# A transformer block on one core: where the pre-added weight sums of a seven-product matrix multiply are made and kept

## The chip, the cores and the metric

The kernel runs on one core of one Trainium2 chip. The metric is the device time of one execution in microseconds (us), as the median of several runs. A core has a matrix engine (TensorE, PE in the profile; its weight loads are PEld), a vector engine (VectorE, DVE), a scalar engine (ScalarE, ACT), a general engine (GpSimd, POOL) and a fifth one that here only issues transfers (SyncE, SP). Each engine works through its own instructions in order and waits on semaphores for the others.

## The reference, cut to what matters

One layer on 256 tokens of width 2048: an input projection, a gated delta rule branch, a sparse attention branch, two sigmoid gates, an output projection, a layer norm, and a gated feed-forward of width 5632 with a second layer norm. All in fp32.

```python
proj = x @ w_in[l]
(qkv_a, a_in, b_in, z, q_b, k_b, v_b, q_i, k_i, w_i, gate_a, gate_b) = jnp.split(proj, offsets, axis=-1)
...
merged = jax.nn.sigmoid(gate_a) * (o_a @ w_branch_a[l]) + jax.nn.sigmoid(gate_b) * (o_b @ w_branch_b[l])
x = layer_norm(DEEPNORM_ALPHA * x + merged @ w_out[l], ln1_g[l], ln1_b[l])
h_gate, h_up = jnp.split(x @ w_ffn_in[l], 2, axis=-1)
x = layer_norm(DEEPNORM_ALPHA * x + (jax.nn.silu(h_gate) * h_up) @ w_ffn_out[l], ln2_g[l], ln2_b[l])
```

## The kernel before

Every weight element is used once, so the weights stream from memory in chunks of 128 x 1024 (512 KB). A chunk is split into a rounded part `hi` (ScalarE, L91) and the remainder `lo` (VectorE, L93); a product with fp32 accuracy is then three matmuls (activations' hi with weights' hi, hi with lo, lo with hi; `mm3`, L217 to L219). Four chunk buffers of each kind (`raw`, `hi`, `lo`) let loading and splitting run ahead of TensorE.

The large projections work on *groups* of 1024 output columns. A group's inner dimension of 2048 is cut into eight *pairs* (numbered q = 0 to 7) of 256 rows. With the 256 tokens as two halves and the 1024 columns as two halves, a pair is a 2 x 2 by 2 x 2 block product. A *plain* pair does its eight block products, 24 matmuls (`plain_pair`). A *seven-product* pair does seven, 21 matmuls (`seven_pair`), after Winograd's form of Strassen's scheme: it needs sums of the weight blocks (`t13`, `t24`: L246, L250, L251 on VectorE), split in turn (L241, L242), and sums of the inputs (`x_form`, made once per q). Four accumulators of the other PSUM pool (`wbank`; the pools `acc` and `aux` have four banks each, and swap roles from group to group) hold the four products that enter several outputs; after the last seven-product pair of a group they are combined (`sums_chain`, L1065 to L1072) and added to the plain ones.

If a pair's weight sums are *ready*, that is made and split earlier, `seven_pair` only needs one and a half chunks split. The sums can be made ready in three ways:

- `early_sums`: just ahead, from the same loads (in z, the gates and the output projection).
- *near*: during group 1 of the feed-forward's first projection (the second large projection stage; groups 1 to 10, tensor `wfg`), for pair 0 of groups 2 and 3, into tiles that group 1 does not need yet (in `f_forms_chain`, four sums by `four_sums`, L934 to L939, and a split, L209).
- *kept*: long ahead, during the first projection (`wws`, `win`), for pair 0 of groups 4 to 7 (`kept_chain`): the two chunks are loaded by SyncE (L948), summed in place, split (L958, L959), and stored by GpSimd's queue to a scratch tensor `d_s` (L961, L962). Before the group that uses them, `kept_load` loads the four tiles back by SyncE (L1415).

Which pairs are seven-product ones: `ZQ` for z, `GQ` for the four gate groups, `FQ` for groups 1 to 10; `ZO`, `GO`, `FO` give the order in which a group takes its pairs, where it is not 0 to 7.

The orders on TensorE and SyncE are written out by hand: they are the order of the program text. Helper work is interleaved by *chains*, generators that `tick` advances at each chunk (a `yield n` waits n ticks, a `yield "name"` an event). The orders on VectorE, ScalarE and GpSimd are chosen when the program is built, by a planner with priorities (`tc.high_priority(offset=LEAD)` raises them; the kept sums have `-LEAD`) and estimated times, and are then fixed.

The stages in order: first projection (to about 356 us; the kept chain runs from `KEPT_FROM` ticks on), z group, gate groups 0 and 1, the attention branch's projection `wbb`, gate groups 2 and 3, the delta branch's projection `wba`, output projection, first layer norm, the feed-forward's first projection (`wfi`, then groups 1 to 10 of `wfg`), its second one (`wfo`), second layer norm.

Of the kernel before, what the change touches and what calls it, by code (L numbers as in the profile page):

```python
# [8 lines left out]
F32 = mybir.dt.float32  # L9
# [8 lines left out]
P = 128  # L18
# [21 lines left out]
GQ = ((2, 4, 6), (0, 2, 4, 6), (0, 2, 4, 6), (0, 2, 4, 6))  # L40
GO = (range(8), (1, 0, 3, 2, 5, 4, 6, 7), (1, 3, 2, 4, 5, 6, 0, 7), (1, 0, 3, 2, 5, 4, 6, 7))
OO = (1, 3, 0, 2, 5, 4, 6, 7)
ZQ = (2, 4, 6)
ZO = (0, 1, 3, 2, 4, 5, 6, 7)
OQ = (0, 2, 4, 6)
WALL = sorted({*WQ[0], *WQ[1]})
KEPT = (4, 5, 6, 7)
NEAR = (2, 3)
FQ = ((4, 6), *[(0, 2, 4, 6) if i in KEPT + NEAR else (2, 4, 6) for i in range(2, 11)])
FO = (1, 3, 2, 0, 4, 5, 6, 7)  # L50
KEPT_FROM = 56
OUT_AT = (8, 9, 10)

LN2_LOAD = (5, 7, 9, 11)
# [9 lines left out]
def block_kernel(ctx: ExitStack, tc: tile.TileContext, xT, x, cpack, onehot, relb, convw, alog, dtb, gnw,  # L64
# [35 lines left out]
    def start(gen, at_once=False):  # L100
        chains.append([gen, clock[0] + (next(gen) if at_once else 0)])
# [17 lines left out]
    def event(name):  # L119
        done[name] = clock[0]  # L120
# [220 lines left out]
    def T(name, shape, dtype=F32, tag=None):  # L341
        return p1.tile(shape, dtype, name=name, tag=tag or name)
# [62 lines left out]
    def need(*names):  # L405
        for n in names:
            assert n in done, n
# [519 lines left out]

    d_s = dr.tile([len(KEPT), 2, P, 2, 1024], F32, name="d_s")

    def four_sums(ra, rb, lead=0):  # L930

        r0, r1, s0, s1 = (t[:, n * 512:n * 512 + 512] for t in (ra, rb) for n in range(2))
        with tc.high_priority(offset=lead):
            nc.vector.tensor_add(r0, r0, s1)  # L934
            nc.vector.tensor_add(s1, r1, s1)
        yield 1
        with tc.high_priority(offset=lead):
            nc.vector.tensor_add(r1, r0, r1)
            nc.vector.tensor_add(s0, r1, s0)  # L939

    def kept_chain():
        yield KEPT_FROM
        raws = [T("k_raw", [P, 2, 1024], tag=t) for t in ("oh_", "s_x")]
        hi = T("k_hi", [P, 2, 1024], F32R, tag="ol_")
        for m, g in enumerate(KEPT):
            raw = raws[m % 2]
            for i in range(2):
                nc.sync.dma_start(raw[:, i], wfg[g - 1, i])  # L948
                yield 1
            yield 1  # L950
            for _ in four_sums(raw[:, 0], raw[:, 1], -LEAD):
                yield 1
            yield 1
            for i in range(2):
                with tc.high_priority(offset=-LEAD):
                    for n in range(2):
                        cs = slice(n * 512, n * 512 + 512)
                        nc.scalar.copy(hi[:, i, cs], raw[:, i, cs])  # L958
                        nc.vector.tensor_sub(raw[:, i, cs].bitcast(F32R), raw[:, i, cs], hi[:, i, cs].bitcast(F32))  # L959
                yield 1  # L960
                nc.gpsimd.dma_start(d_s[m, 0, :, i], hi[:, i].bitcast(F32))  # L961
                nc.gpsimd.dma_start(d_s[m, 1, :, i], raw[:, i])  # L962
        event("kept")

    start(kept_chain())
    conv_first(s_kT, pss)
    event("kc0")
    for dst, h0, c0, ev in ((s_kT, 4, 12, "kc1"), (s_qT, 0, 0, "qc0"), (s_qT, 4, 4, "qc1"),
# [24 lines left out]
    def z_chain():  # L993

        yield "v1"
        yield 1
        need("kept")
        t0 = [rp.tile([P, 2, 1024], F32R, name=f"z_t{i}", tag=f"x1_{i}") for i in range(2)]
        wt = two("z_wt", F32, "ol_")
        gates_home.update(wraw=halves(two("z_wraw", F32, "oh_")), wt=halves(wt), thi=halves(t0[0]), tlo=halves(t0[1]))  # L1000
        for q, old in ((4, "s_ak"), (6, "s_sq")):
            t = T(f"g_form{q}", [P, 2, 4, P], F32R, tag=old)
            gates_form[q] = t[:, 0], t[:, 1]
        gates_form[2] = [p1.tile([P, 4, P], F32R, name="g_form2", tag="rel", bufs=2) for _ in range(2)]
        yield from early_sums(wz, ZQ[0], home, z_ready)
        yield 1
        x_form(ZQ[0], gates_form[ZQ[0]], wt[:, 0, :512], wt[:, 0, 512:])
        yield "lg"
        t1 = two("z_t2", F32R, "s_vT"), two("z_t3", F32R, "s_t")
        for tag, *t in zip(("thi", "tlo"), t0, t1):  # L1010
            gates_home[tag] = halves(*t)
            gates_home[tag][0] = 2
        yield from early_sums(wz, ZQ[1], home, z_ready)
        for q in ZQ[1:]:
            yield 1
            x_form(q, gates_form[q], wt[:, 0, :512], wt[:, 0, 512:])
        event("zready")
# [30 lines left out]
    def next_sets(*olds):  # L1048
        for tag, old in zip(("thi", "tlo"), olds):
            e = gates_home[tag]  # L1050
            gates_home[tag] = [0, e[1][:2] + halves(two("h_" + old, F32R, old))[1]]
# [88 lines left out]

    def ga_rows():
        if "a" not in g_rows:
            next_sets("s_x", "s_mn")
            g_rows["a"] = [rp.tile([P, D], F32, name=f"ga{tb}", tag=f"x1_{tb}") for tb in range(NTB)]
        return g_rows["a"]
# [4 lines left out]
    token_block(vb, 1)  # L1150
    event("vb")
    need("lg", "o", "mask")
    z_group()
    event("z")
    gates_buffers()
    start(late_form(0))
    for i in range(2):
        gate_group(gb_rows, i)
    gb = gb_rows()
    for tag in ("thi", "tlo"):  # L1160
        gates_home[tag][0] = 0
    start(early_chain(wgt[2], (2, 4), ga_ready, "gaready"))
    for j in range(4):
        js = slice(j * 512, (j + 1) * 512)
        for tb, ps in enumerate(block_xs([wbb[j, k] for k in range(4)], *out_hl, ps_acc if j == 2 else ps_aux)):
            nc.vector.tensor_mul(gb[tb][:, js], ps, gb[tb][:, js])
# [85 lines left out]
    def fetch(i, j):  # L1252
# [1 line left out]
        nc.sync.dma_start(t.rearrange("p k t -> p (k t)").bitcast(F32), d_h[i, j])  # L1254

    h_first = passing()
    near = [[hp_.tile([P, 1024], F32R if i > 1 else F32, name="near", tag=f"{hl}{i}") for hl in ("hH", "hL")]
            for i in range(1, 5)]
    l1 = ExitStack()
    gp = l1.enter_context(tc.tile_pool(name="gp1", bufs=1, side="left", reuse_waits="tile"))  # L1260
    ex = l1.enter_context(tc.tile_pool(name="ex1", bufs=4, side="left", reuse_waits="tile"))
# [71 lines left out]
    def fv():  # L1333
        return fp.tile([P, 512], F32, name="v", tag="v", bufs=4)
# [20 lines left out]
                  lambda tb, ps: start(h_chain(0, tb, gated(tb, ps), ps_aux)))  # L1355
    l1.close()
    hp2 = fh.enter_context(tc.tile_pool(name="hp2", bufs=1, side="left", reuse_waits="tile"))
    near.append([hp2.tile([P, 1024], F32R, name="near", tag=f"{hl}5") for hl in ("hH", "hL")])
    kept = [None, [hp2.tile([P, 1024], F32R, name="kept", tag=f"{hl}6") for hl in ("hH", "hL")]]


    f_home = {}
# [13 lines left out]
    def f_forms_chain():  # L1376
        yield "x1"
        for tb in range(NTB):
            yield 2
            nc.sync.dma_start(d_x1[tb], x1[tb])  # L1380
        t = [rp.tile([P, 2, 2, 4, P], F32R, name="f_form", tag=f"x1_{tb}") for tb in range(NTB)]
        for i, q in enumerate((4, 6, 2, 0)):
            yield 1
            f_form[q] = t[i // 2][:, i % 2, 0], t[i // 2][:, i % 2, 1]
            x_form(q, f_form[q], fv(), fv())
        yield 1
        raw = near[0]
        for m, g in enumerate(NEAR):
            for i in range(2):
                nc.sync.dma_start(raw[i], wfg[g - 1, i])  # L1390
                yield 1
            yield 1
            yield from four_sums(*raw)
            for i in range(2):
                yield 1
                split(near[1 + 2 * m][i], near[2 + 2 * m][i], raw[i])
            k_ready[g][0] = sums_of(near[1 + 2 * m], near[2 + 2 * m])
            yield 4

    k_ready = {g: {} for g in KEPT + NEAR}  # L1400

    def sums_of(hi, lo):
        (t1, t2), (t4, t3) = ([(hi[i][:, n * 512:n * 512 + 512], lo[i][:, n * 512:n * 512 + 512]) for n in range(2)]
# [3 lines left out]
    def kept_load(m):  # L1407

        for i in range(2):
            if m or not i:  # L1410
                kept[i] = [hp2.tile([P, 1024], F32R, name="kept", tag=f"{hl}{5 + i}") for hl in ("hH", "hL")]
            for j in range(2):
                if i or j:
                    yield 3
                nc.sync.dma_start(kept[i][j].bitcast(F32), d_s[m, j, :, i])  # L1415
        k_ready[KEPT[m]][0] = sums_of(*zip(*kept))

# [47 lines left out]
    for i in range(1, NG + 1):  # L1465
        std, shared = (ps_aux, ps_acc) if i % 2 else (ps_acc, ps_aux)
        sums = []

        def places():
            sums.extend(fv() for _ in range(4))  # L1470
            return sums

        at = {6: lambda: start(kept_load(KEPT.index(i + 1)))} if i + 1 in KEPT else {}
        ready = k_ready.get(i)
        if ready is not None:
            at[0] = lambda ready=ready: ready[0]
        bank = x_group(wfg[i - 1], FQ[i - 1], std, shared, f_form, fhome, lambda wbank: sums_chain(places(), wbank),
                       at, range(8) if ready is None else FO, {} if ready is None else ready)
        if i == NEAR[-1]:
            for k in range(1, 5):  # L1480
                h_tile(hp_, k)
        if i == KEPT[-1]:
            for k in (5, 6):
                h_tile(hp2, k)
        if i == NG:
            h_tile(hp2, 7)
        start(hidden_chain(i, bank, sums, std), at_once=True)
# [258 lines left out]
```

## Time and profile before

| | us |
|---|---|
| median of 3 runs | 1454.04 (1452.1 to 1454.48) |
| the profiled execution, whole | 1454.49 |
| its span on the core | 1452.7 |
| TensorE busy | 1443.7 |
| VectorE busy | 1279.0 |
| ScalarE busy | 813.9 |

The profile is of one execution. "Span" is from its first to its last instruction. Rows of the timeline give the start in us, the duration, engine, line of the kernel and operation; "x2" is the number of instructions in one row. Rows of the grouped view give the number of instructions, their busy time, the mean duration in ns, and the idle time of the engine just before them with what ended it. A row of a stretch of time gives its length and the busy us of PE, PEld, DVE, ACT and POOL with instruction counts, then the granted clock, the transfers' share and GB/s. Matmuls are pipelined, so the duration shown for one is longer than the step from one to the next.

### The profile page before, as it was taken

What the parts mean: (1) busy time and instruction counts of PE and PEld (TensorE: products, weight loads), DVE (VectorE), ACT (ScalarE), POOL (GpSimd) and SP (SyncE); (2) the same over time, 40 slices, a digit from 0 to 9 for tenths busy, and PEclk for the clock granted to TensorE, in tenths of its full rate; (3) what the DMA queues carried; (4) which work ended last, traced back from release to release, by engine and by line L of the source; (5) the groups of instructions that cost most, each with busy time, mean ns of one, the idle gap of its engine ahead of it and who ended that gap; (6) DMA issues with size and microseconds to landing.
All of it is one profiled execution on the core that took longest, in us unless ns stands there. A gap on an engine that the chain in (4) does not pass through costs nothing.

```text
span 1452.7 us, 19640 instructions
## 1 busy us (share of the span) xinstructions
PE 1443.7 (99%) x7140; PEld 1213.8 (84%) x7140; DVE 1279.0 (88%) x1763; ACT 813.9 (56%) x1021; POOL 56.2 (4%) x75
## 2 busy tenths in 40 slices
PE   9999999999999999999999999999999999999998
PEld 8888888888888888888888878888888888888887
DVE  6798988789699959998886999989999998989987
ACT  5765454557456646655435665656566565554552
POOL 0002011121000000000000000000000000000000
PEclk9999999999999999999999999999999999999999
DMA  8646589854556755756856767777766666887863
GB/s 293 197 159 196 175 216 335 295 187 151 169 198 232 233 193 198 247 188 204 304 202 218 264 236 253 251 271 255 279 211 212 216 215 247 311 342 265 315 215 118
DMA packets 101969, 336.40 MB, mean 232 GB/s; under 512 B 17696, under 2 KB 18888, under 8 KB 101360
## 3 DMA queue, kind: packets, MB, share of 16 engines
q1 hardware_dynamic: 88512, 310.03, 62.0%
q0 software_dynamic: 6176, 22.75, 4.6%
q10 hardware_dynamic: 7184, 2.36, 0.7%
q8 instruction: 56, 0.92, 0.2%
q14 instruction: 41, 0.34, 0.1%
HBM read 312.88 MB, written 22.22 MB: 231 GB/s over the span
## 4 chain that ended last, share of the span: by engine, by line
PE 92%; DVE 3%; DMA 3%; issue 1%; ACT 1%; SPq 0%; POOLq 0%; DVEq 0%; ACTq 0%
PE acc L217 10%; PE acc L218 10%; PE acc L219 10%; PE acc L153 10%; PE aux L218 9%; PE aux L217 9%; PE aux L219 9%; PE acc L156 5%; PE acc L175 3%; PE acc L173 3%; PE acc L174 3%; PE aux L173 2%; PE aux L174 1%; PE aux L175 1%; DMA raw<-in_win_dram 1%; PE aux L737 1%
## 5 line engine op out<-in xcount | busy, mean ns | idle before, releaser
L91 ACT CAST hi<-raw 128x1024 fp32r<-128x1024 f32 (+1 forms) x388 | 396.9, 1032 | 345.3 <-PE acc L219 87.3
L93 DVE TENSOR_TENSOR lo<-raw,hi 128x1024 fp32r<-128x1024 f32 (+1 forms) x388 | 463.5, 1205 | 87.3 <-ACT hi L91 84.7
L153 PE MATMUL acc<-X,hi 128*128 128x512 f32 x640 | 203.7, 400 | 0.0
L217 PE MATMUL acc<-hi,X 128*128 128x512 f32 x369 | 145.0, 393 | 0.8 <-DVE v L1072 0.8
L156 PEld LDWEIGHTS acc<-X,lo 128*128 128x128 f32 x640 | 120.2, 188 | 28.3
L219 PE MATMUL acc<-hi,X 128*128 128x512 f32 x369 | 143.7, 389 | 0.0
L218 PE MATMUL acc<-lo,X 128*128 128x512 f32 x369 | 143.6, 389 | 0.0
L156 PE MATMUL acc<-X,lo 128*128 128x256 f32 x640 | 126.0, 278 | 0.0
L217 PE MATMUL aux<-hi,X 128*128 128x512 f32 x313 | 122.4, 391 | 0.0
L219 PE MATMUL aux<-hi,X 128*128 128x512 f32 x313 | 121.9, 389 | 0.0
L218 PE MATMUL aux<-lo,X 128*128 128x512 f32 x313 | 121.8, 389 | 0.0
L153 PEld LDWEIGHTS acc<-X,hi 128*128 128x128 f32 x640 | 97.5, 189 | 2.0 <-ACT hi L91 0.7
L241 ACT CAST f_thi<-f_wt 128x1024 fp32r<-128x1024 f32 x58 | 61.0, 1053 | 46.4 <-DVE f_wt L251 23.9
L217 PEld LDWEIGHTS acc<-hi,X 128*128 128x128 f32 x369 | 69.3, 188 | 15.9 <-DVE v L1072 1.2
L219 PEld LDWEIGHTS acc<-hi,X 128*128 128x128 f32 x369 | 69.3, 188 | 14.5
L218 PEld LDWEIGHTS acc<-lo,X 128*128 128x128 f32 x369 | 69.3, 188 | 13.9
L242 DVE TENSOR_TENSOR f_tlo<-f_wt,f_thi 128x1024 fp32r<-128x1024 f32 x58 | 70.6, 1220 | 6.2 <-ACT f_thi L241 6.1
L219 PEld LDWEIGHTS aux<-hi,X 128*128 128x128 f32 x313 | 58.8, 188 | 12.3
L218 PEld LDWEIGHTS aux<-lo,X 128*128 128x128 f32 x313 | 58.8, 188 | 12.1
L217 PEld LDWEIGHTS aux<-hi,X 128*128 128x128 f32 x313 | 58.8, 188 | 12.0
L241 ACT CAST thi<-wt 128x1024 fp32r<-128x1024 f32 x36 | 37.9, 1054 | 49.0 <-DVE wt L246 31.6
L173 PE MATMUL acc<-hi,X 128*128 128x512 f32 x160 | 64.3, 402 | 0.0
(681 smaller groups left out, 3123.6 us busy)
## 6 DMA issues: line engine op xcount, KB each, us to landing
raw<-in_wfg_dram SPq DMA_DIRECT2D x125, 512.0 KB, 4.8
raw<-in_wws_dram SPq DMA_DIRECT2D x80, 512.0 KB, 4.1
raw<-in_wfo_dram SPq DMA_DIRECT2D x70, 512.0 KB, 5.0
raw<-in_wgt_dram SPq DMA_DIRECT2D x49, 512.0 KB, 3.9
f_wraw<-in_wfg_dram SPq DMA_DIRECT2D x29, 512.0 KB, 6.2
raw<-in_win_dram SPq DMA_DIRECT2D x21, 512.0 KB, 4.1
wraw<-in_wfo_dram SPq DMA_DIRECT2D x18, 512.0 KB, 5.1
gt<-d_g SPq DMA_DIRECT2D x18, 512.0 KB, 6.8
```

The costliest lines, as they stand in the source:

```text
L91: nc.scalar.copy(hi, raw)
L93: nc.vector.tensor_sub(lo, raw, hi.bitcast(F32))
L153: nc.tensor.matmul(pss[c], hv[:, kk, cs[c]], X2[k // 4][:, k % 4], start=(k == 0), stop=False, skip_group_check=True)
L156: nc.tensor.matmul(pss[c][:, :S], lv[:, kk, cs[c]], xh[:, k, :], start=False, stop=(k == KT - 1), skip_group_check=True)
L173: nc.tensor.matmul(ps, xh, hv[:, kk], start=(k == 0), stop=False)
L174: nc.tensor.matmul(ps, xh, lv[:, kk], start=False, stop=False)
L175: nc.tensor.matmul(ps, xl, hv[:, kk], start=False, stop=(k == 2 * n - 1))
L217: nc.tensor.matmul(o, sh, hi, start=first, stop=False)
L218: nc.tensor.matmul(o, sh, lo, start=False, stop=False)
L219: nc.tensor.matmul(o, sl, hi, start=False, stop=last)
L241: nc.scalar.copy(hi, v)
L242: nc.vector.tensor_sub(lo, v, hi.bitcast(F32))
```

## The change

z has four seven-product pairs instead of three, with another order, and the form of input 0 is made during z instead of after it. Group 1 has three instead of two, with an order of its own. The near sums are gone: group 2 has no ready pair and three seven-product pairs instead of four, and group 3's pair 0 becomes a kept one, so that five groups (3 to 7) have one. Four of the five are kept in the first projection, starting four ticks earlier; the fifth (group 7) runs beside `wbb`, in one raw tile and one `hi` tile. The first of each four kept sums multiplies its operand by a column of ones that SyncE loads just then, two ticks after the second raw tile. The input forms of the feed-forward get buffers of their own.

```diff
-ZQ = (2, 4, 6)
-ZO = (0, 1, 3, 2, 4, 5, 6, 7)
+ZQ = (2, 4, 0, 6)
+ZO = (1, 3, 5, 2, 4, 0, 6, 7)
...
-KEPT = (4, 5, 6, 7)
-NEAR = (2, 3)
-FQ = ((4, 6), *[(0, 2, 4, 6) if i in KEPT + NEAR else (2, 4, 6) for i in range(2, 11)])
+KEPT = range(3, 8)
+FQ = [(0, 2, 4, 6) if i in KEPT else (2, 4, 6) for i in range(1, 11)]
+F1 = (1, 3, 4, 5, 6, 0, 2, 7)
 FO = (1, 3, 2, 0, 4, 5, 6, 7)
-KEPT_FROM = 56
+KEPT_FROM = 52
...
-    def four_sums(ra, rb, lead=0):
+    def four_sums(ra, rb, lead, one):
...
-            nc.vector.tensor_add(r0, r0, s1)
+            nc.vector.scalar_tensor_tensor(r0, r0, one, s1, op0=OP.mult, op1=OP.add)
             nc.vector.tensor_add(s1, r1, s1)
...
-    def kept_chain():
-        yield KEPT_FROM
-        raws = [T("k_raw", [P, 2, 1024], tag=t) for t in ("oh_", "s_x")]
-        hi = T("k_hi", [P, 2, 1024], F32R, tag="ol_")
-        for m, g in enumerate(KEPT):
-            raw = raws[m % 2]
+    def kept_chain(ms, wait, old, old_hi, gap, ev):
+        yield wait
+        raws = [T(f"k_raw{t}", [P, 2, 1024], tag=t) for t in old]
+        hi = T(f"k_hi{old_hi}", [P, 2, 1024], F32R, tag=old_hi)
+        for m in ms:
+            if gap and m > ms[0]:
+                yield gap
+            raw = raws[m % len(old)]
             for i in range(2):
-                nc.sync.dma_start(raw[:, i], wfg[g - 1, i])
+                nc.sync.dma_start(raw[:, i], wfg[KEPT[m] - 1, i])
                 yield 1
             yield 1
-            for _ in four_sums(raw[:, 0], raw[:, 1], -LEAD):
+            one = sm.tile([P, 1], F32, name="one", tag="one", bufs=2)
+            nc.sync.dma_start(one, cpack[:, C_ONE:C_ONE + 1])
+            for _ in four_sums(raw[:, 0], raw[:, 1], -LEAD, one):
                 yield 1
...
-    start(kept_chain())
+    start(kept_chain(range(4), KEPT_FROM, ("oh_", "s_x"), "ol_", 0, "kept0"))
...
-        for q in ZQ[1:]:
+        for q in ZQ[1::2]:
...
     def ga_rows():
         if "a" not in g_rows:
+            need("kept1")
...
+    start(late_form(0))
     z_group()
     event("z")
     gates_buffers()
-    start(late_form(0))
...
     start(early_chain(wgt[2], (2, 4), ga_ready, "gaready"))
+    start(kept_chain(range(4, 5), 1, ("s_x",), "s_rv", 5, "kept1"))
...
-    near = [[hp_.tile([P, 1024], F32R if i > 1 else F32, name="near", tag=f"{hl}{i}") for hl in ("hH", "hL")]
-            for i in range(1, 5)]
+    room = [[hp_.tile([P, 1024], F32, name="room", tag=f"{hl}{i}") for hl in ("hH", "hL")] for i in range(1, 5)]
...
-            x_form(q, f_form[q], fv(), fv())
-        yield 1
-        raw = near[0]
-        for m, g in enumerate(NEAR):
-            for i in range(2):
-                nc.sync.dma_start(raw[i], wfg[g - 1, i])
-                yield 1
-            yield 1
-            yield from four_sums(*raw)
-            for i in range(2):
-                yield 1
-                split(near[1 + 2 * m][i], near[2 + 2 * m][i], raw[i])
-            k_ready[g][0] = sums_of(near[1 + 2 * m], near[2 + 2 * m])
-            yield 4
+            x_form(q, f_form[q], *(t[:, :512] for t in room[i]))
...
-                       at, range(8) if ready is None else FO, {} if ready is None else ready)
+                       at, F1 if i == 1 else range(8) if ready is None else FO, {} if ready is None else ready)
```

More of the change, by code (lines that the diff above doesn't have):

```diff
@@ L962, in kept_chain @@
                 nc.gpsimd.dma_start(d_s[m, 1, :, i], raw[:, i])
-        event("kept")
-    start(kept_chain())
+        event(ev)
+    start(kept_chain(range(4), KEPT_FROM, ("oh_", "s_x"), "ol_", 0, "kept0"))
     conv_first(s_kT, pss)
@@ L996, in z_chain @@
         yield 1
-        need("kept")
+        need("kept0")
         t0 = [rp.tile([P, 2, 1024], F32R, name=f"z_t{i}", tag=f"x1_{i}") for i in range(2)]
@@ L1357, in block_kernel @@
     hp2 = fh.enter_context(tc.tile_pool(name="hp2", bufs=1, side="left", reuse_waits="tile"))
-    near.append([hp2.tile([P, 1024], F32R, name="near", tag=f"{hl}5") for hl in ("hH", "hL")])
-    kept = [None, [hp2.tile([P, 1024], F32R, name="kept", tag=f"{hl}6") for hl in ("hH", "hL")]]
+    kept = [[hp2.tile([P, 1024], F32R, name="kept", tag=f"{hl}{5 + i}") for hl in ("hH", "hL")] for i in range(2)]
     f_home = {}
@@ L1384, in f_forms_chain @@
             f_form[q] = t[i // 2][:, i % 2, 0], t[i // 2][:, i % 2, 1]
-            x_form(q, f_form[q], fv(), fv())
-        yield 1
-        raw = near[0]
-        for m, g in enumerate(NEAR):
-            for i in range(2):
-                nc.sync.dma_start(raw[i], wfg[g - 1, i])
-                yield 1
-            yield 1
-            yield from four_sums(*raw)
-            for i in range(2):
-                yield 1
-                split(near[1 + 2 * m][i], near[2 + 2 * m][i], raw[i])
-            k_ready[g][0] = sums_of(near[1 + 2 * m], near[2 + 2 * m])
-            yield 4
-    k_ready = {g: {} for g in KEPT + NEAR}
+            x_form(q, f_form[q], *(t[:, :512] for t in room[i]))
+    k_ready = {g: {} for g in KEPT}
     def sums_of(hi, lo):
@@ L1409, in kept_load @@
         for i in range(2):
-            if m or not i:
+            if m:
                 kept[i] = [hp2.tile([P, 1024], F32R, name="kept", tag=f"{hl}{5 + i}") for hl in ("hH", "hL")]
@@ L1477, in block_kernel @@
         bank = x_group(wfg[i - 1], FQ[i - 1], std, shared, f_form, fhome, lambda wbank: sums_chain(places(), wbank),
-                       at, range(8) if ready is None else FO, {} if ready is None else ready)
-        if i == NEAR[-1]:
+                       at, F1 if i == 1 else range(8) if ready is None else FO, {} if ready is None else ready)
+        if i == 1:
             for k in range(1, 5):
```

## The prediction

> **What bounds the kernel now.** I read the page's busy shares first, then the waits of TensorE, then the chain that ended last, then the busy time by stage.
>
> ```profile
> PE 1443.7 (99%) x7140; PEld 1213.8 (84%) x7140; DVE 1279.0 (88%) x1763; ACT 813.9 (56%) x1021; POOL 56.2 (4%) x75
> PE acc L136 <- ACT hi L91: 1.2, 1, 1.2
> PE aux L421 <- DVE warm L417: 1.1, 1, 1.1
> PE acc L139 <- DVE lo L93: 0.9, 2, 0.6
> PE acc L217 <- DVE v L1072: 0.8, 1, 0.8
> PE aux L1623 <- ACT ct L1617: 0.7, 1, 0.7
> PE aux L617 <- ACT s_t L623: 0.4, 1, 0.4
> ```
>
> TensorE (PE) is busy for 1443.7 of 1452.7 us. The six rows after it are all of its waits that have a releaser (waited for, total, times, longest): 5.1 us together. Those at L136, L421 and L139 belong to the start and L1623 to the end, where the change does nothing. Only 0.8 us (L217) and 0.4 us (L617) lie where it reaches. So a saving can come from fewer matmuls and from these 1.2 us; anything larger would have to be a loss, from a wait that is not there yet. VectorE (DVE) at 88% is the engine that could make one.
>
> The price of a pair of row blocks taken with seven products instead of eight can be read off the chain. In every group of the second projection, line 1435 transposes at the same place, so two neighbouring starts enclose one group's matmuls:
>
> ```profile
> 845.63 0.87 PE aux L1435 x8
> 887.33 0.87 PE acc L1435 x8
> ...
> 1138.27 0.87 PE acc L1435 x8
> 1180.67 0.87 PE aux L1435 x8
> ```
>
> Between groups with four seven-product pairs the step is 887.33 - 845.63 = 41.70 us; between groups 8 to 10, which have three, it is 1180.67 - 1138.27 = 42.40 us. One seven-product pair is therefore worth 0.7 us (three matmuls: 21 instead of 24), with no wait in either kind of group.
>
> **The change, part by part.**
>
> *Matmuls.* The z group gets a fourth such pair (0.7 us less), group 1 a third (0.7 less), group 2 loses its fourth (0.7 more), groups 3 to 7 keep four and 8 to 10 three. Net 0.7 us less.
>
> *The near sums go away.* Groups 2 and 3 had their first pair's sums made during group 1. The chain of the page shows what that did at group 1's end:
>
> ```profile
> 829.27 3.49 DVE lo L93 x3
> 832.76 1.14 DVE near L209
> ...
> 838.47 0.70 DVE v L1072
> 839.21 0.50 PE acc L217
> ```
>
> Here TensorE's work is released by L1072 of VectorE, the last of the sums that empty group 1's four banks; they stand behind a near split (L209) and three chunk remainders (L93). That is the 0.8 us. Each near group costs VectorE four half-width sums and two full splits:
>
> ```profile
> L934 DVE TENSOR_TENSOR near<-near 128x512 f32<-128x512 f32 x2 | 1.4, 688 | 3.1 <-DMA near<-in_wfg_dram 3.1
> L209 DVE TENSOR_TENSOR near<-near 128x1024 fp32r<-128x1024 f32 x4 | 4.9, 1220 | 0.0
> L242 DVE TENSOR_TENSOR f_tlo<-f_wt,f_thi 128x1024 fp32r<-128x1024 f32 x58 | 70.6, 1220 | 6.2 <-ACT f_thi L241 6.1
> L246 DVE TENSOR_TENSOR f_wt<-f_wraw,raw 128x1024 f32<-128x1024 f32 x29 | 35.3, 1218 | 0.0
> L250 DVE TENSOR_TENSOR f_wt<-f_wt,f_wraw 128x512 f32<-128x512 f32 x29 | 19.9, 686 | 0.1
> L93 DVE TENSOR_TENSOR lo<-raw,hi 128x1024 fp32r<-128x1024 f32 x371 | 451.8, 1229 | 80.8 <-ACT hi L91 78.3
> 793.00:838.00 45.00, 44.99 (x201) 36.97 (x200) 44.44 (x59) 27.14 (x33) 1.13 (x2) 1.00 0.74 251
> ```
>
> 4 x 0.69 + 2 x 1.22 = 5.2 us, twice 10.4 us, all inside group 1 where VectorE is busy 44.44 of 45.00 us (last row: PE, PEld, DVE, ACT, POOL busy). Its 3.1 us wait for the near load goes too. Against that, group 1's third pair with sums made on the spot costs VectorE 2 x 1.22 (L242) + 1.22 (L246) + 2 x 0.69 (L250 and the like L251) + 1.22 + 0.69 (remainders of one and a half chunks) = 6.9 us, where a plain pair costs 2 x 1.23 = 2.5: 4.4 more. Group 2's pair 0, plain again, costs 0.5 more. Net 5.5 us less VectorE work in a stretch that is short of it by 0.8. I book the 0.8 us as gained; the ends are 0 and 0.8. Next in line behind those bank sums is nothing that is late: groups 8 to 10 end the same way, with three pairs made on the spot at the same places, and have no wait.
>
> *Group 1's order.* Its first seven-product pair moves from place 5 to place 3 and needs its four banks earlier. The fourth was last read by the second of two splits:
>
> ```profile
> 793.31 0.39 PE L217 MATMUL aux<-hi,X 128*128 128x512 f32 x1
> 801.28 1.22 DVE L209 TENSOR_TENSOR near<-near 128x1024 fp32r<-128x1024 f32 x1
> 803.75 1.22 DVE L209 TENSOR_TENSOR near<-near 128x1024 fp32r<-128x1024 f32 x1
> 809.30 0.42 DVE L209 TENSOR_TENSOR pass<-acc,pass 128x256 fp32r<-128x256 f32 x1
> 815.54 0.39 PE L217 MATMUL acc<-hi,X 128*128 128x512 f32 x1
> ```
>
> Four pairs and a set of transposes lie between 793.31 and 815.54, so a pair is some 5.4 us; two pairs and the 0.6 us of transposes later is 804.7, and the fourth bank is wanted nine of a pair's 24 matmuls after that (2.0 us), near 806.7. The split ended at 809.72: 3.0 us too late if nothing else moved. But the two near splits ahead of it (2.4 us), the near sums and two input forms (about 2 us each, which now get buffers of their own and can run before the group) leave that queue. I take 0; the ends are 0 and 3.0.
>
> *The z group.* Two pairs with sums made on the spot now follow each other (0, then 6): 13.8 us of VectorE in 2 x (5.4 - 0.7) = 9.4 us of TensorE (5.4 is worked out above), a deficit of 4.4. With the form of input 0 (two half-width and four quarter instructions, about 2.5 us) pulled in ahead, VectorE gets 6.9 us more:
>
> ```profile
> 356.30:404.50 48.20, 48.20 (x241) 40.58 (x240) 32.10 (x40) 22.72 (x30) 0.00 (x0) 1.00 0.54 182
> 404.50:446.00 41.50, 41.50 (x185) 34.38 (x184) 40.70 (x57) 27.10 (x29) 0.00 (x0) 1.00 0.63 215
> 446.00:484.00 38.00, 38.00 (x170) 31.46 (x169) 37.85 (x43) 24.68 (x30) 0.00 (x0) 1.00 0.64 212
> 484.00:530.00 46.00, 46.00 (x205) 38.10 (x204) 34.62 (x37) 22.95 (x24) 0.00 (x0) 1.00 0.65 209
> ```
>
> The z stretch (first row) has 16.1 us of idle VectorE, and the two pairs before 0 are ready ones that need little. The gate group at 446 to 484 already has two such pairs in a row (4, then 6), with VectorE at 37.85 of 38.00, and TensorE does not wait. I take 0; the ends are 0 and 4.4. The first gate group (second row) loses the 2.5 us of the form.
>
> *The kept groups.* Four of five stay in the first stage, started four steps earlier; the fifth runs beside the attention branch's projection (last row: 11.4 us of idle VectorE for its 5.2, SyncE's two loads, four stores on GpSimd's queue). Its tiles are wanted in the third gate group, after 530. Group 3 now loads four kept tiles as groups 4 to 7 do, which have no wait, and four near loads go from the same SyncE queue. All 0.
>
> *The sums tied to a loaded one.* The first of each four sums becomes a scalar_tensor_tensor: 0.746 against 0.688 us by the rows of its kind, 5 x 0.06 = 0.3 us of VectorE, hidden. The new thing is a load of 128 single elements, five times, two chunks behind the raw tiles in SyncE's queue; VectorE takes its work in order, so while it waits for the one, all chunk remainders and bank copies queue behind it, and TensorE waits for those.
>
> ```profile
> L1286 DVE SCALAR_TENSOR_TENSOR x<-x,rs,lnb 128x512 f32<-128x512 f32 x8 | 5.8, 746 | 0.0
> gnw<-in_gnw_dram SPq DMA_DIRECT2D x1, 0.5 KB, 2.5
> DMA to landing us min/median/max: 4.6/7.3/8.4
> 251.63 0.69 DVE L934 TENSOR_TENSOR k_raw<-k_raw 128x512 f32<-128x512 f32 x1 [3.34 <-DMA k_raw<-in_wfg_dram]
> ```
>
> The nearest load of that shape took 2.5 us; loads of kept tiles (third row) took up to 8.4. VectorE already lost 3.34 us in one go to such a load (last row), and the whole stage cost TensorE 0.4 us (L617). So a wait up to 3.3 us is absorbed. A later place in SyncE's order may also put the sums behind the landing and save that 0.4. Ends: 0.4 gained, and 8.4 - 3.3 = 5.1 lost for each sum that meets a full queue. I take 0, since 2.5 is the nearest row.
>
> [...]
>
> **Sum.** 0.7 + 0.8 = 1.5 us less. The profiled execution took 1454.49 us (span 1452.7 and 1.8 around it), which gives 1453.0; the median of the runs is 1454.04, 0.45 lower, which gives 1452.5. That is 0.10%, and about 0.2% (2.9 us) is what a measurement of this kernel can tell from no change.
>
> **Rivals.**
> - *A kept sum waits for its one, and TensorE with it (slower).* Place: the kept sums of the first stage, of which one now waits near 251 us. For it: the 3.34 us wait and DMA landings of 8.4 us there. Against: only 0.4 us reached TensorE. One exposed load: 1452.5 + 5.1 = 1457.6 us. It decides once a wait is longer than some 3.3 + 1.5 + 2.9 = 7.7 us.
> - *VectorE runs behind in z.* 1452.5 + 4.4 = 1456.9 us if the 16.1 us of idle time cannot be used, because the buffers of the sums come free only pair by pair. Against: the gate group with the same two neighbours.
> - *Group 1's wait is moved, not removed.* The fourth bank is late by up to 3.0 us and the 0.8 returns: 1452.5 + 0.8 + 3.0 = 1456.3 us at the worst, 1453.3 if only the 0.8 stays. For it: VectorE is 99% busy in that group. Against: 5.5 us of its work are gone.
> - *More than the sum.* The early chain moves out of a crowded stretch and L617's 0.4 us goes as well: 1452.1. Beyond 2.9 us it would need waits that no view shows.
>
> **How the numbers follow.** My forecast (between 1452.1 and 1453.3, the 0.4 and the 0.8 as its own range) has a chance of 0.64. The one exposed gets 0.10, z behind 0.08 (half of it reaches beyond no change), group 1's moved wait 0.10 (a third beyond), a gain past 0.2% 0.08. Slower by over 0.2% then has 0.10 x 0.7 + 0.04 + 0.03 = 0.14, faster 0.08, and the rest, 0.78, is within. The range starts 1.1 us under 1452.1, since single runs lie 1.9 us under and 0.4 over their median, and goes up to 1456.0, which takes in most of the two VectorE rivals but not an exposed load.
>
> **What would show it.** TensorE should have 21 matmuls in pair 0 of z and three seven-product pairs in group 1; the wait of L217 for the sums of group 1 should be gone, and the step from group 2's transposes to group 3's be near 42.4 instead of 41.70. The wait list should have no new row of over 1 us between 40 and 1440 us. It goes wrong if VectorE shows an idle time of over 7 us before the first kept sum, if a row "acc" of group 1 waits for a split at L209 near 806, or if z's second pair made on the spot starts late.

## The result, and the profile after

| | before | after |
|---|---|---|
| median, us | 1453.7 (1452.1 to 1454.48) | 1470.76 (1468.22 to 1471.6) |
| ratio to before | | 1.0116, interval 1.0098 to 1.0133 |
| the profiled execution, whole | 1454.49 | 1471.6 |
| its span | 1452.7 | 1469.7 |

The changed kernel is 17.1 us slower; 1452.5 was forecast, with 1456.0 as the upper end. First the busy shares and the waits of TensorE after:

```profile
PE 1457.3 (99%) x7137; PEld 1215.2 (83%) x7137; DVE 1285.3 (87%) x1769; ACT 814.7 (55%) x1025; POOL 58.3 (4%) x79
```

```profile
PE acc L217 <- ACT s_u L981: 2.6, 1, 2.6
PE acc L139 <- DVE lo L93: 1.5, 2, 0.8
PE acc L174 <- DVE lo L93: 1.2, 1, 1.2
PE aux L421 <- DVE warm L417: 1.1, 1, 1.1
PE aux L737 <- DVE s_rv L765: 1.1, 1, 1.1
PE aux L1614 <- ACT ct L1608: 0.7, 1, 0.7
```

Three matmuls fewer, as planned (7137 for 7140), and yet TensorE is *busy* 13.6 us longer (1457.3 against 1443.7). Waits add nothing to the busy time: most of the loss sits inside the matmuls. Three rows of waits are new (L981, L174, L765; 4.9 us), and the wait for the sums of group 1 is gone.

The transposes that close each group (L1426 now) show the same in the chain of the work that ended last:

```profile
854.79 0.87 PE aux L1426 x8
897.41 0.87 PE acc L1426 x8
939.40 0.87 PE aux L1426 x8
...
1192.63 0.87 PE aux L1426 x8
1235.49 0.87 PE acc L1426 x8
```

A group with four seven-product pairs takes 939.40 - 897.41 = 41.99 us (41.70 before), one with three 1235.49 - 1192.63 = 42.86 (42.40 before), with no wait in either. In the last projection, the groups of matmuls by operation give a mean duration of 394 ns after, and 389 before (first row after, second before, the stretch from 1260 to 1420 us):

```profile
L217 PE MATMUL acc<-hi,hH 128*128 128x512 f32 x77 | 30.3, 394 | 0.0
```

```profile
L217 PE MATMUL aux<-hi,hH 128*128 128x512 f32 x67 | 26.1, 389 | 0.0
```

Taken over the whole timeline (start of a 512-column matmul to the start of the next matmul, steps under 0.3 us), the mean is 227.64 ns over 5392 steps before and 229.89 over 5388 after: 2.25 ns x 5388 = 12.1 us. By what a matmul reads, before and after: products with `hH`, `hL` and `gt` 226.8 and 232.0, attention and delta outputs (`oh_`, `ol_`) 227.3 and 233.3, input forms 226.7 and 230.3, plain products with X 227.1 and 227.8, the first projection at L153 233.0 and 233.0.

The granted clock is not the reason: its mean is 0.998 after and 0.999 before, and between 40 and 1440 us it is 1.00 but for one stretch (rows of 350 to 360, 360 to 365 and 365 to 370 us after: length, busy PE, PEld, DVE, ACT, POOL, clock, DMA share, GB/s):

```profile
350.00:360.00 10.00, 8.78 (x47) 7.14 (x46) 9.97 (x19) 8.33 (x22) 0.00 (x0) 1.00 0.35 108
360.00:365.00 5.00, 2.35 (x10) 1.57 (x9) 4.96 (x10) 2.54 (x4) 0.00 (x0) 1.00 0.82 292
365.00:370.00 5.00, 5.00 (x20) 4.16 (x19) 3.04 (x6) 2.05 (x3) 0.00 (x0) 0.66 0.42 115
```

That stretch (5 us at 0.66, so 1.7 us lost) belongs to the second part of the loss. VectorE's timeline has one wait for a loaded one, and long waits behind it; the last row is the landing time of the five loads:

```profile
269.45 0.75 DVE L934 SCALAR_TENSOR_TENSOR k_raws_x<-k_raws_x,one 128x512 f32<-128x512 f32 x1 [4.60 <-DMA one<-in_cpack_dram]
287.33 0.69 DVE L1061 TENSOR_TENSOR f_room<-X 128x512 f32<-128x512 f32 x1 [5.86 <-DMA d_s<-k_raws_x]
301.81 1.23 DVE L246 TENSOR_TENSOR z_wt<-z_wraw 128x1024 f32<-128x1024 f32 x1 [6.45 <-DMA z_wraw<-in_wz_dram]
```

```profile
DMA to landing us min/median/max: 4.7/5.6/12.2
```

### The profile page after: what moved, and what is told of

It reads as the page before. It is cut to its first block, busy times and chain, and to the rows that moved or that the text cites. A ratio compares the mean times of both kernels' runs of the same rounds, so it can differ in the third digit from the quotient of the medians.

```text
span 1469.7 us, 19652 instructions
## 1 busy us (share of the span) xinstructions
PE 1457.3 (99%) x7137; PEld 1215.2 (83%) x7137; DVE 1285.3 (87%) x1769; ACT 814.7 (55%) x1025; POOL 58.3 (4%) x79
## 4 chain that ended last, share of the span: by engine, by line
PE 75%; ACT 0%; DVE 0%; POOLq 0%; issue 0%
PE acc L218 11%; PE acc L217 11%; PE acc L219 11%; PE aux L218 10%; PE aux L219 10%; PE aux L217 10%; PE acc L173 3%; PE acc L175 3%; PE acc L174 2%; PE aux L175 2%; PE aux L174 2%; PE aux L173 2%; PE aux L1124 0%; PE aux L895 0%; PE acc L1426 0%; PE aux L1426 0%
## 5 line engine op out<-in xcount | busy, mean ns | idle before, releaser
L91 ACT CAST hi<-raw 128x1024 fp32r<-128x1024 f32 (+1 forms) x384 | 392.4, 1032 | 325.2 <-PE acc L219 74.4
L153 PE MATMUL acc<-X,hi 128*128 128x512 f32 x640 | 203.7, 400 | 0.0
L217 PE MATMUL acc<-hi,X 128*128 128x512 f32 x370 | 146.0, 395 | 2.6 <-ACT s_u L981 2.6
L218 PE MATMUL acc<-lo,X 128*128 128x512 f32 x370 | 144.8, 391 | 0.0
L217 PE MATMUL aux<-hi,X 128*128 128x512 f32 x306 | 119.6, 391 | 0.0
L218 PE MATMUL aux<-lo,X 128*128 128x512 f32 x306 | 119.5, 390 | 0.0
L219 PE MATMUL aux<-hi,X 128*128 128x512 f32 x306 | 119.2, 390 | 0.0
L153 PEld LDWEIGHTS acc<-X,hi 128*128 128x128 f32 x640 | 97.5, 189 | 2.0 <-ACT hi L91 0.7
L217 PEld LDWEIGHTS acc<-hi,X 128*128 128x128 f32 x370 | 69.9, 189 | 17.6 <-ACT s_u L981 3.1
L218 PEld LDWEIGHTS acc<-lo,X 128*128 128x128 f32 x370 | 69.9, 189 | 14.5
L218 PEld LDWEIGHTS aux<-lo,X 128*128 128x128 f32 x306 | 57.5, 188 | 12.3 <-DVE lo L93 0.4
L217 PEld LDWEIGHTS aux<-hi,X 128*128 128x128 f32 x306 | 57.5, 188 | 12.1
L174 PE MATMUL acc<-lo,X 128*128 128x512 f32 x160 | 62.4, 390 | 1.2 <-DVE lo L93 1.2
```

The costliest lines, as they stand in the source:

```text
L91: nc.scalar.copy(hi, raw)
L153: nc.tensor.matmul(pss[c], hv[:, kk, cs[c]], X2[k // 4][:, k % 4], start=(k == 0), stop=False, skip_group_check=True)
L174: nc.tensor.matmul(ps, xh, lv[:, kk], start=False, stop=False)
L217: nc.tensor.matmul(o, sh, hi, start=first, stop=False)
L218: nc.tensor.matmul(o, sh, lo, start=False, stop=False)
L219: nc.tensor.matmul(o, sl, hi, start=False, stop=last)
```

## The experiments

Two suspects, then. **Addresses**: the two buffers of `one` are allocated among the small tiles of the left side, 2 x 32 bytes, and every left-side tile behind them moves by 64 bytes. The compiled programs give (bytes within a partition):

```
                             before            after
weight chunks raw/hi/lo        8832 ...          8832 ...   (128 modulo 256, both)
s_kT, f_form                  58752             58816       (128, then 192)
hH0                           75136             75200       (128, then 192)
X (right side)               196480            196480       (128, both)
```

An unused tile `pads` stands in the same column, so its length moves those tiles and nothing else. **Waits**: VectorE waiting for the ones.

### Addresses alone

`e1_after_addr`: the changed kernel with its tiles back at the old places.

```diff
-    pads = sm.tile([P, 56], F32, name="pads")
+    pads = sm.tile([P, 40], F32, name="pads")
```

> The changed kernel with its unused tile 'pads' 64 bytes smaller, so that every tile behind the two small 'one' tiles stands at the address it had before; the instructions of all engines and their order stay. Addresses (theory A): the step of 512-column matmuls goes back from 229.9 to 227.6 ns, about 11 us less: 1459 to 1460 us, and the waits near 311, 350 and 361 us stay. Waits alone (theory B, all of the 17 us come from VectorE standing behind transfers, and the longer step is a consequence of it): 1470 to 1471 us.

Measured: 1458.8 us (1457.41 to 1462.77), ratio to before 1.0037 (1.0023 to 1.005), a step of 227.66 ns. 12.0 us of the 17 go with 64 bytes; every order of instructions is that of the changed kernel, and the waits are left. The trace is of the slowest of five executions (1462.77 us), which behind the start has one wait more than the kernel after, at L218:

```profile
PE acc L217 <- ACT s_u L981: 2.6, 1, 2.6
PE acc L174 <- DVE lo L93: 1.3, 1, 1.3
PE aux L218 <- DVE lo L93: 1.1, 1, 1.1
PE aux L737 <- DVE s_rv L765: 0.9, 1, 0.9
```

`e2_before_addr64`: the kernel before, with 64 bytes added (`pads` of 72).

> The kernel before with 'pads' 64 bytes larger and nothing else changed. Theory A: the step rises to about 230 ns, 1464 to 1466 us. Theory B: 1454 us, as before.

Measured: 1465.88 us, ratio 1.0079 (1.0064 to 1.0094), a step of 229.87 ns. The loss comes without any of the change; the chain's step between groups is that of after, 933.17 - 891.18 = 41.99 us:

```profile
891.18 0.87 PE acc L1435 x8
933.17 0.88 PE aux L1435 x8
```

`e3_before_addr128`: the same with 128 bytes (`pads` of 88).

> The kernel before with 'pads' 128 bytes larger. Theory A with a period of 128 bytes: 1454 us, step 227 ns. Theory A with a longer period (the good addresses stand at 384 modulo 512): some of the loss of the 64-byte shift, up to 1466 us. Theory B: 1454 us.

Measured: 1468.07 us, ratio 1.0096 (1.008 to 1.0113), a step of 230.46 ns. So 128 bytes are no period.

`e5_before_addr512`: with 512 bytes (`pads` of 184).

> The kernel before, with every left-side tile behind the small ones 512 bytes higher (no instruction changed). Theory A1 (the matmul step depends on where its operands stand within a period of at most 512 bytes): nothing changes, 1454.6 us within 0.2%, a mean step of 227.6 ns for 512 columns, as against +11.3 us at 64 bytes and +13.5 at 128. Rival A2 (the old place is special, any move costs): 1466 to 1468 us, a step near 230 ns.

Measured: 1454.54 us, ratio 1.0 (0.999 to 1.0009), 227.64 ns. Not every move costs.

`e10_before_addr256`: with 256 bytes (`pads` of 120).

> The kernel before with every left-side tile behind the small ones 256 bytes higher (no instruction changed). If the step repeats every 256 bytes (the first projection did not change when its weight chunks moved by 256): 1454.4 us within 0.2% and a step of 227.6 ns. If it repeats only every 512: 1460 us or more, a step of 229 to 231 ns, as at 64 and 128 bytes.

Measured: 1453.99 us, ratio 0.9993 (0.9982 to 1.0005), 227.63 ns. At 256 bytes, as at 512, the step is that of the kernel before.

### Which place, or whose

These start from the changed kernel without the ones (`e4_after_no_one`, below: 1452.93 us, 227.63 ns).

`e6_no_one_weights_addr256`: the weight chunks 256 bytes higher.

```diff
-    ident = cst.tile([P, P], F32, name="ident")
+    ident = cst.tile([P, P + 64], F32, name="ident")[:, :P]
...
-    pads = sm.tile([P, 56], F32, name="pads")
+    pads = sm.tile([P, 120], F32, name="pads")
```

> The changed kernel without the ones, and with the weight chunk buffers 256 bytes higher, from 128 to 384 modulo 512, all tiles behind them 512 bytes higher. Theory A (it is the stationary operand's address: 384 modulo 512 gives 227 ns, others up to 233): the first projection's matmuls at L153, the only 512-column ones whose stationary operand is a weight chunk, go from 233.0 to 227 ns; 609 of them, so 3.7 us less: 1452.9 - 3.7 = 1449.2 us. Other classes keep 227. Rival (it is the moving operand's address, or how the two stand to each other): the other classes, whose moving operand is a weight chunk, change from 227 towards 230 to 233, 1465 us or more. Rival 2 (the 233 ns of L153 come from its mix with 256-column matmuls): nothing changes, 1452.9 us.

Measured: 1453.06 us, ratio 0.9993 (0.9984 to 1.0003); L153 stays at 233.0 ns. The theory of a bad place of the chunks missed its 3.7 us. A period of 256 was one reading left, with which `e10_before_addr256` then agreed (227.63 ns) for the tiles behind the chunks. The other, that L153's 233.0 ns come from its mix with matmuls of 256 columns, fits as well and was not tried by itself.

`e9_no_one_weights_addr64`: the weight chunks alone 64 bytes higher (`ident` of P + 16, `pads` of 168).

> The changed kernel without the ones; the weight chunk buffers 64 bytes higher (192 modulo 256 instead of 128), everything behind them 512 bytes higher, so only the weight chunks change their place. Theory S (the stationary operand's address decides): the classes that have weight chunks as the moving operand (products with X, with forms, with oh and ol) keep 226.7 to 227.3 ns; only the first projection, where chunks are stationary, may change, by at most some 6 ns on 609 + 640 matmuls: 1453 us, 7 more at most. Theory M (the moving operand's address decides): X (2562 steps) and the rest with chunks as moving operand (378 + 696) go to about 230 to 233 ns, 3636 steps by 3 to 6 ns, 11 to 22 us more: 1464 to 1475 us, and the first projection keeps 233.0.

Measured: 1463.24 us, ratio 1.0066 (1.0049 to 1.0083), a mean of 229.81 ns; products with X 229.4, with forms 231.0, with `oh_` and `ol_` 229.1, L153 231.1 (faster by 1.9). Neither theory holds: the products with X and with `oh_` and `ol_` went up less than theory M said, and the first projection changed too, downwards.

`e11_no_one_all_addr64` and `e12_no_one_all_addr128`: all large tiles together, left and right, to 192 and to 0 modulo 256.

```diff
-    ident = cst.tile([P, P], F32, name="ident")
+    ident = cst.tile([P, P + 16], F32, name="ident")[:, :P]     # e12: P + 32
...
-    pad = padp.tile([P, 24], F32, name="pad")
+    pad = padp.tile([P, 8], F32, name="pad")                    # e12: 56
```

> The changed kernel without the ones, with every large tile on both sides 64 bytes further: all of them at 192 modulo 256 instead of all at 128. Theory R (a matmul is slower where tiles used at the same time stand at different places modulo 256, whatever the place): 1452.9 us within 0.2%, a mean step of 227.6 ns, 227.1 for products with X. Theory P (the place itself counts, 128 is the good one): 1463 us or more, a step of 229.5 ns or more.

> The same with all large tiles at 0 modulo 256. Theory R (only differences count): 1452.9 us within 0.2%, 227.6 ns. Theory P (the place itself counts): another time, 1463 us or more with a step of 229.5 ns or more if 128 is the only good place; if 0 is a better one, less than 1450 us with a step under 227.0 ns.

Measured: 1452.91 us, ratio 0.9988 (0.9979 to 0.9998), and 1453.17 us, ratio 0.9988 (0.9977 to 0.9999); steps of 227.60 and 227.63 ns. The first one's chain is back at 927.36 - 885.66 = 41.70 us a group:

```profile
885.66 0.87 PE acc L1425 x8
927.36 0.87 PE aux L1425 x8
```

The whole picture, with the place modulo 256 of the weight chunks, the other left-side tiles, and X:

| kernel | chunks / left / X | mean step, ns | median, us |
|---|---|---|---|
| before, and with 512 or 256 bytes | 128 / 128 / 128 | 227.64, 227.64, 227.63 | 1454.62, 1454.54, 1453.99 |
| before + 64, before + 128 | 128 / 192 / 128, 128 / 0 / 128 | 229.87, 230.46 | 1465.88, 1468.07 |
| after, after at the old places | 128 / 192 / 128, 128 / 128 / 128 | 229.89, 227.66 | 1470.76, 1458.8 |
| no one, chunks + 64 | 192 / 128 / 128 | 229.81 | 1463.24 |
| no one; all + 64; all + 128 | all 128; all 192; all 0 | 227.63, 227.60, 227.63 | 1452.93, 1452.91, 1453.17 |

For the mean step the place itself does not count (0, 128 and 192 were tried); that the tiles stand at the same one does.

### The ones

`e4_after_no_one`: the changed kernel with plain sums and no `one` tiles (the tiles stand at the old places by themselves).

```diff
-            nc.vector.scalar_tensor_tensor(r0, r0, one, s1, op0=OP.mult, op1=OP.add)
+            nc.vector.tensor_add(r0, r0, s1)
...
-            one = sm.tile([P, 1], F32, name="one", tag="one", bufs=2)
-            nc.sync.dma_start(one, cpack[:, C_ONE:C_ONE + 1])
```

> The changed kernel with plain additions in the kept sums and without the 'one' tiles and their loads, so that all addresses are those of before and no kept sum waits for a one. Theory A with the one's wait (4.6 us on VectorE) as the source of the waits of 300 to 370 us: 1453 to 1455 us. Theory A with the waits coming from other parts (the z group, the store of the kept tiles): 1457 to 1460 us. Theory B with the one as its only source: 1453 us as well, and then e1 tells them apart.

Measured: 1452.93 us (1451.39 to 1458.01), ratio 0.9989 (0.9978 to 1.0001). Against `e1_after_addr`, at the same addresses, the ones cost 1458.8 - 1452.93 = 5.9 us by the medians. VectorE's timeline without them, where the rows after stood at 269.45, 287.33 and 301.81:

```profile
262.95 0.69 DVE L934 TENSOR_TENSOR k_raws_x<-k_raws_x 128x512 f32<-128x512 f32 x1 [2.38 <-DMA k_raws_x<-in_wfg_dram]
279.22 0.69 DVE L1060 TENSOR_TENSOR f_room<-X 128x512 f32<-128x512 f32 x1 [4.18 <-DMA d_s<-k_raws_x]
296.23 1.23 DVE L246 TENSOR_TENSOR z_wt<-z_wraw 128x1024 f32<-128x1024 f32 x1 [2.58 <-DMA z_wraw<-in_wz_dram]
```

VectorE is late by 6.5, 8.1 and 5.6 us, and it does not catch up before z, though it idles more: behind the late sums it waits for their store (5.86 us, 4.18 without the ones) and then for z's load (6.45 and 2.58). There the lag reaches TensorE through ScalarE. The timelines after (four rows of the input form, ScalarE and TensorE), then without the ones (two rows):

```profile
361.32 0.28 DVE L314 TENSOR_TENSOR z_wt<-z_wt 128x128 f32<-128x128 f32 x1
361.64 0.62 ACT L208 CAST g_form<-z_wt 128x512 fp32r<-128x512 f32 x1 [2.19 <-DVE z_wt L314]
363.58 0.59 ACT L981 COPY s_u<-acc 128x512 f32<-128x512 f32 x1
364.22 0.49 PE L217 MATMUL acc<-hi,X 128*128 128x512 f32 x1 [2.65 <-ACT s_u L981]
```

```profile
355.01 0.29 DVE L314 TENSOR_TENSOR z_wt<-z_wt 128x128 f32<-128x128 f32 x1
357.28 0.59 ACT L980 COPY s_u<-acc 128x512 f32<-128x512 f32 x1
```

ScalarE took its work in order here: the cast of an input form (L208) waits for VectorE's L314, 6.3 us late, and the copy that empties a bank for z (L981) stands behind that cast, with a chunk's cast (362.16) and another copy (363.11) between them. TensorE idles 2.65 us for the bank, and then the clock drops to 0.66 (365 to 370 us):

```profile
366.98 0.63 PE L219 MATMUL acc<-hi,X 128*128 128x512 f32 x1
367.40 0.63 PE L217 MATMUL acc<-hi,X 128*128 128x512 f32 x1
...
369.10 0.39 PE L218 MATMUL acc<-lo,X 128*128 128x512 f32 x1
369.33 0.40 PE L219 MATMUL acc<-hi,X 128*128 128x512 f32 x1
```

Steps of 0.42 us instead of 0.23 for some seven matmuls are 7 x 0.2 = 1.4 us more; the 1.7 us by the granted clock take in the small matmuls among them. Here the clock fell behind an idle gap of 2.65 us; in `e8_before_one` below it stayed at 1.00 behind one of 2.61 us, and what makes it fall is not shown. The same gap at L217 cost more in `e1_after_addr` (rows of 360 to 365 and 365 to 370 us), 5 x 0.18 + 5 x 0.50 = 3.4 us:

```profile
360.00:365.00 5.00, 2.35 (x8) 1.60 (x8) 4.93 (x11) 2.54 (x4) 0.00 (x0) 0.82 0.84 292
365.00:370.00 5.00, 5.00 (x18) 4.12 (x17) 2.64 (x4) 2.05 (x3) 0.00 (x0) 0.50 0.24 66
```

`e7_after_addr_one_early`: `e1_after_addr` with each one loaded ahead of its two raw tiles.

```diff
+            one = sm.tile([P, 1], F32, name="one", tag="one", bufs=2)
+            nc.sync.dma_start(one, cpack[:, C_ONE:C_ONE + 1])
             raw = raws[m % len(old)]
             for i in range(2):
                 nc.sync.dma_start(raw[:, i], wfg[KEPT[m] - 1, i])
                 yield 1
             yield 1
-            one = sm.tile([P, 1], F32, name="one", tag="one", bufs=2)
-            nc.sync.dma_start(one, cpack[:, C_ONE:C_ONE + 1])
```

> The changed kernel with the old addresses, and each column of ones loaded ahead of its two raw tiles instead of behind them; the tied sums stay. Theory B (the 5.9 us between the two versions at the old addresses come from the late landing of the ones, which stalls VectorE in order): no wait of VectorE for a one, TensorE's waits near 311, 350 and 361 us go, 1453 us (1451.5 to 1454.5). Rival (the instruction with the ones, or the other order of VectorE that it leads to): the waits at 311 to 361 stay and the time is 1457 to 1459 us.

Measured: 1452.56 us, ratio 0.9989 (0.998 to 0.9998). The tied sums stay and cost nothing; VectorE now waits for the raw tile, and the ones' landings are shorter:

```profile
263.78 0.75 DVE L934 SCALAR_TENSOR_TENSOR k_raws_x<-k_raws_x,one 128x512 f32<-128x512 f32 x1 [3.09 <-DMA k_raws_x<-in_wfg_dram]
```

```profile
DMA to landing us min/median/max: 3.4/4.4/4.9
```

So the loss was the late landing of the ones, not the tied instruction.

`e8_before_one`: the kernel before with the ones of the change in its kept sums, tiles at the old places (`pads` of 40).

> The kernel before, with the ones and the tied sums added to its kept chain as the change has them, tiles at the old addresses; near sums, z and group 1 as before. Theory B (the load of the ones is enough by itself): VectorE waits 3 to 5 us for a one, TensorE gets new waits of 1 to 3 us each between 300 and 370 us, and the time is 1457 to 1461 us. Rival (it needs the other parts of the change as well, the earlier start of the kept chain and the fourth pair of z): VectorE waits but TensorE does not, 1454.6 us within 0.2%.

Measured: 1459.71 us (1457.2 to 1460.2), ratio 1.0037 (1.0022 to 1.0051). The ones are enough without the rest of the change, and with two short waits (rows of VectorE, then TensorE's wait, then the clock in 365 to 370 us):

```profile
254.33 0.75 DVE L937 SCALAR_TENSOR_TENSOR k_raw<-k_raw,one 128x512 f32<-128x512 f32 x1 [1.54 <-DMA one<-in_cpack_dram]
278.23 0.75 DVE L937 SCALAR_TENSOR_TENSOR k_raw<-k_raw,one 128x512 f32<-128x512 f32 x1 [1.73 <-DMA one<-in_cpack_dram]
360.34 0.50 PE L217 MATMUL acc<-hi,X 128*128 128x512 f32 x1 [2.61 <-ACT s_u L982]
```

```profile
365.00:370.00 5.00, 5.00 (x24) 4.14 (x23) 2.42 (x2) 2.10 (x2) 0.00 (x0) 1.00 0.50 157
```

The expectation of several TensorE waits missed: there is one. In this profiled execution, the shortest of the five, the clock stayed at 1.00; the other four took 1459.1 to 1460.2 us at a mean clock of 0.998 or 0.999. They have no trace here, so whether the clock fell behind the wait of 2.6 us in those four is not shown.

## Why the prediction was wrong, point by point

- **A term was missing.** The sum priced instructions, loads and waits, and the prediction took it that anything larger "would have to be a loss, from a wait that is not there yet". That step failed: the larger part of the loss came with no wait. That two 4-byte tiles move all the tiles allocated behind them was in no step. It cost 12.0 us (after against `e1_after_addr`), about the same on the unchanged kernel (11.3 us, `e2_before_addr64`), and it explains a longer busy time with fewer matmuls.
- **The load of the ones was taken at 0, with 2.5 us per landing as the nearest row.** Measured landings were 4.7 to 12.2 us, so the stage's own loads (up to 8.4) were nearer than the small load from elsewhere. The cost was 5.9 us. The end of the range of that step, 5.1, was short by 0.8; the rival that rested on it (1457.6 us) comes within 1.2 us of what was measured at the old addresses, 1458.8.
- **"A wait up to 3.3 us is absorbed" failed.** It read the slack off one wait. In `e8_before_one` VectorE waits 1.5 and 1.7 us for a one, less in sum than the 3.3 and 1.5 us that the kernel before waits for raw tiles at the same two sums. But the sums start 254.33 - 251.63 = 2.7 and 278.23 - 274.17 = 4.1 us later (the second figure before is in the row below), and that reached TensorE as 2.6 us. Idle time nearby did not make the delay good, since what follows waits for the late sums' own store (2.8 us at L246 in that trace). It is paid where something urgent is queued behind late work, here the bank copies some 80 to 105 us later. For the same reason a wait of 7.7 us was not needed.

```profile
274.17 0.69 DVE L934 TENSOR_TENSOR k_raw<-k_raw 128x512 f32<-128x512 f32 x1 [1.54 <-DMA k_raw<-in_wfg_dram]
```

- **The matmuls came out as priced.** Without the ones and at one place, group 2 takes 42.38 us and groups with four pairs 41.72 (chain of `e4_after_no_one`):

```profile
843.05 0.87 PE aux L1425 x8
885.43 0.87 PE acc L1425 x8
927.15 0.88 PE aux L1425 x8
```

- **Group 1's 0.8 us came, and L617's 0.4 too.** 843.05 stands 2.58 us ahead of the 845.63 before: 0.7 of z, 0.7 of group 1, 0.8 and 0.4 make 2.6. That the total fits so closely is partly luck. At the transposes near 671 us (L1120 before, L1123 here) the lead is 671.21 - 670.15 = 1.06 us, as booked; at those inside group 1 (L1347 and L1351) only 801.48 - 800.84 = 0.64, and the rest of group 1 brings 1.94 where 1.5 was booked. All TensorE waits listed between 20 and 1440 us in that kernel are these:

```profile
PE acc L156 <- DVE lo L93: 0.4, 1, 0.4
PE aux L1123 <- issue: 0.2, 1, 0.2
```

- **Group 1's order, two pairs made on the spot in z, and the kept groups cost nothing**, as taken: neither of the two rows above belongs to them.
- **The sum of 1.5 us holds for the change without the ones**: 1452.93 against 1454.62 for the kernel before in the same series, 1.7 us less; its interval (0.9978 to 1.0001) takes in no change. With it the parts add up: 12.0 + 5.9 - 1.7 = 16.2 of the 17.1 us, and the rest is the kernel before itself, at 1453.7 us beside the kernel after and at 1454.62 in this series. Three versions beat the kernel before by their intervals, all by 0.1%: `e7_after_addr_one_early`, which keeps the tied sums, and `e11_no_one_all_addr64` and `e12_no_one_all_addr128`, which drop them.
- **What would show it** named a VectorE wait of over 7 us before the first kept sum; the wait was 4.6 us and before the fourth. The test for a new TensorE row of over 1 us caught this part; the longer step, which is 12.0 us of the loss, shows only faintly in what was named: from group 2's transposes to group 3's it was 897.41 - 854.79 = 42.62 us where 42.4 was expected.

## What to carry to other kernels

A new tile, however small, can be a move of every tile allocated behind it (two of 4 bytes a partition moved the left-side ones by 64 bytes here): compare the addresses of the matmul operands before and after a change, and where TensorE is busy longer with no more matmuls, look there first. In a matmul-bound kernel like this one, keep all large operands at one place modulo 256 bytes, with a pad if need be (a mean step of 227.6 ns here, for 229.8 to 230.5). Issue a small load that an in-order engine will wait for ahead of the large ones it accompanies (landings of 3.4 to 4.9 us here, for 4.7 to 12.2), and price a delay on such an engine by what waits for its results later, not by the idle time nearby.

## What the runs showed of the hardware

The 512-column matmuls of these runs (on split parts of type fp32r) stepped at 227.6 ns on average when the chunks, the other left-side tiles and X started at the same place modulo 256 bytes (0, 128 and 192 were tried), and at 229.8 to 230.5 when they did not. One of the classes that lost most, the chunks' `hi` with input forms of the feed-forward (70 matmuls), went from 226.7 to 237.7 ns at 128 bytes (`e3_before_addr128`; a group with four seven-product pairs took 42.2 us there, for 41.7). Over some 5390 matmuls the mean makes 12 to 15 us; the medians rose by 11.3 (64 bytes) and 13.5 us (128 bytes). TensorE's step changed by 11 ns in that class with nothing but addresses changed.

What makes the step longer is not shown by any run. It is not only the two operands of one matmul: in `e9_no_one_weights_addr64`, where the chunks alone moved, products of the feed-forward's split weight sums (`f_thi`) with its input forms went from 226.7 to 233.6 ns, though both operands stayed at 128. And not every product with a moved chunk suffers: chunk remainders `lo` with X went from 226.8 to 227.2 ns there, and in the last projection `lo` with `hH` kept its mean duration of 389 ns, where `hi` with `hH` went to 394. The places of what ScalarE and VectorE read and write at that time were not varied by themselves. Open, too, is why L153 steps at 233.0 ns wherever all stand alike.
